# Norm row work on VectorE and ScalarE alone, whole last products, and a mixer that begins with seven gate pairs

## The chip, the cores and the metric

The kernel runs on one core of a Trainium2 chip. The time is device microseconds of one execution; a kernel's time is the median of its runs. Engines are named as in the profile: PE (TensorE matmul), PEld (its weight load), DVE (VectorE), ACT (ScalarE), POOL (GpSimd) and SP (SyncE, which issues most DMAs).

## The reference

One layer on x of 1 x 1024 tokens x 1024 (float32), cut to what is computed:

```python
def rms_norm(x, g):
    y = x * lax.rsqrt(jnp.mean(x * x, axis=-1, keepdims=True) + EPS)
    return y * g

def swiglu_ffn(x, w_in, w_out):                  # D_FF = 2816
    gate, up = jnp.split(x @ w_in, 2, axis=-1)
    return (jax.nn.silu(gate) * up) @ w_out

x = x + 0.5 * swiglu_ffn(rms_norm(x, ffn1_norm), ffn1_w_in, ffn1_w_out)
u = rms_norm(x, mix_norm)
q_a, k_a, v_a, q_b, k_b, v_b, gate_logits = jnp.split(u @ w_mix_in, SPLITS, axis=-1)
y_a = chunked_band_attention(q_a, k_a, v_a, rel_bias_a)        # 8 heads of 64, band of 576 keys
y_b = diff_attention(q_b, k_b, v_b, t5_bias, lam, ...)         # 4 heads, two softmaxes each, rms_norm
g_a, g_b = jnp.split(jax.nn.sigmoid(gate_logits + b_gate), 2, axis=-1)
merged = g_a * (y_a @ w_branch_a) + g_b * (y_b @ w_branch_b)
x = x + merged @ w_o
x = x + 0.5 * swiglu_ffn(rms_norm(x, ffn2_norm), ffn2_w_in, ffn2_w_out)
out = rms_norm(x, final_norm)
```

## The kernel before

Every float32 operand of a large product is split in two parts, "hi" (an ACT cast, L95) and "lo" (a DVE subtraction, L100), and a product is three matmuls, hi·hi, hi·lo and lo·hi (`mm3`, L124). The large projections use the Strassen-Winograd scheme of seven products of half-size blocks (`PRODUCTS`, L167): the activations' sums are made once per norm, the weights' sums (T1, T2, T3, N4) as they are needed.

The stages, one after the other: norm; FFN1-in (22 `Pair`s of columns, seven products of 12 matmuls each, every matmul 128x512); FFN1-out (`out_projection`: seven products `P1` to `P7`, each over 11 blocks i and 4 token tiles, 132 matmuls); norm; mixer-in (16 pairs, and the two `project_v`); attention (branch A with 8 heads, branch B with 4, the projection of A as a filler); the projection of B; W_o (the same `out_projection`, 4 blocks); norm; FFN2-in; FFN2-out; final norm.

The order on each engine is a list scheduler's: the program text gives the priority, data and free buffers the readiness, and each engine then runs its list in order. Buffers are rings: `raw` (RAW = 6 tiles of 4 KB per partition: weights as loaded, rows x, attention's probabilities), `unit` (WU = 18 tiles of 2 KB: the hi and lo parts, and the rows `xc`), `temp` (TF = 10), `wtemp` (TT = 3); one buffer holds the norm's gain or the tables' rows (tag `gain`).

A norm between two stages (`renorm`, L524) has eight rows of 128 tokens. Rows 0 to 3 are done while the last product of the projection runs (`early`): squares on ACT, the power on POOL (`rsqrt`, L137), the scaling on DVE (L201), then `put`: four PE transposes, an ACT cast and a DVE subtraction. Rows 4 to 7 come with the last product (`late`): the same, and for each row four sums of halves on POOL (`norm1a`, L220 to L223), whose results are transposed (S1, S2, S4); the gain of the right half is multiplied in on POOL (L187). While this lasts, the PE has the "heads" of the next stage: products 0 and 2 of a pair, which need only rows 0 to 3 (A11 and A12). Five pairs are begun that way; then the rest of pair 0 starts with T1·S1, which needs all eight rows. In the mixer the pairs 0 to 7 make queries and keys, the pairs 8 to 15 the gates.

With `by_pairs` (W_o and FFN2-out) the last product goes over the token tiles two by two: all blocks i for tokens 4 and 5, then all again for 6 and 7, so that the first two rows can be finished early. Each weight block is split twice, and the activation block in halves of 128x256 whose subtraction is POOL's (L467). In FFN2-out, `finish2` (L1000 on) does the final norm of rows 0 to 3 during it and of rows 4 to 7 behind it.

`setup` (L576 on) makes the two bias tables: POOL loads ea, negates and stretches it, writes `diag_a` with eight DMAs (L613), then `diag_b` with four and four. All of it is called once, at pair 4 of FFN1-in (L386). FFN_ORDER (L398) is the order of the seven products of FFN-out.

Of the kernel before, what the change touches and what calls it, by code (L numbers as in the profile page):

```python
# [9 lines left out]
F32 = mybir.dt.float32  # L10
# [34 lines left out]
RAW, WU, TF, TT = 6, 18, 10, 3  # L45
# [7 lines left out]
def hybrid_layer_kernel(ctx, tc, x, ffn1_norm, ffn1_w_in, ffn1_w_out, mix_norm, w_mix_in,  # L53
# [33 lines left out]
    junk = const.tile([P, HALF], mybir.dt.bfloat16, name="junk")  # L87
# [59 lines left out]
    def rstd_row(xt):  # L147

        ssq = small.tile([P, 2], F32, tag="ssq", name="ssq")
        for d in range(2):  # L150
            nc.scalar.activation(out=junk, in_=xt[d], func=AF.Square,
                                 scale=D ** -0.5, accum_out=ssq[:, d:d + 1])
        v = small.tile([P, 1], F32, tag="v", name="v")
        nc.vector.scalar_tensor_tensor(out=v, in0=ssq[:, 0:1], scalar=EPS, in1=ssq[:, 1:2],
                                       op0=ALU.add, op1=ALU.add)
        return rsqrt(v)

# [16 lines left out]
    class Row:  # L174


        def __init__(self, x):
            self.x, self.gained = x, [None, None]
            self.ssq = small.tile([P, 2], F32, tag="rsq", bufs=10, name="rsq")

        def take(self, d, gain, on_pool):

            nc.scalar.activation(out=junk, in_=self.x[d], func=AF.Square, scale=D ** -0.5,  # L183
                                 accum_out=self.ssq[:, d:d + 1])
            g = gain[:, d * HALF:(d + 1) * HALF]
            if on_pool:
                nc.gpsimd.tensor_tensor(out=self.x[d], in0=self.x[d], in1=g, op=ALU.mult)  # L187
            else:
                self.gained[d] = g

        def scale(self):
# [5 lines left out]
            for d in range(2):  # L197
                if self.gained[d] is None:
                    nc.scalar.activation(out=self.x[d], in_=self.x[d], func=AF.Copy, scale=r)
                else:  # L200
                    nc.vector.scalar_tensor_tensor(out=self.x[d], in0=self.x[d], scalar=r, in1=self.gained[d],  # L201
                                                   op0=ALU.mult, op1=ALU.mult)
# [8 lines left out]
    def norm0(t, row0, u, ps):  # L211

        for d, name in enumerate(("A11", "A12")):
            put(u, name, t, row0.x[d], ps)

    def norm1a(t, row0, row1, u, ps):

        (a11, a12), (a21, a22) = row0.x, row1.x
        s1 = temp([P, HALF], "s1")
        nc.gpsimd.tensor_tensor(out=s1, in0=a21, in1=a22, op=ALU.add)  # L220
        nc.gpsimd.tensor_tensor(out=a21, in0=a11, in1=a21, op=ALU.subtract)
        nc.gpsimd.tensor_tensor(out=a11, in0=s1, in1=a11, op=ALU.subtract)
        nc.gpsimd.tensor_tensor(out=a12, in0=a12, in1=a11, op=ALU.subtract)  # L223
        put(u, "S1", t, s1, ps)
        put(u, "S2", t, a11, ps)
        put(u, "S4", t, a12, ps)

    def norm1b(t, row1, u, ps):

        put(u, "S3", t, row1.x[0], ps)  # L230
        put(u, "A22", t, row1.x[1], ps)
# [22 lines left out]
    class Combine:  # L254


        def __init__(self, ps, shape, sink):
            self.ps, self.shape, self.sink, self.held, self.chains = ps, shape, sink, {}, {}

        def acc(self, m):  # L260

            name = PRODUCTS[m][2]
# [8 lines left out]
        def after(self, m, p):  # L271
# [9 lines left out]
            if m in (0, 1, 3):  # L281
# [14 lines left out]
    class Pair:  # L296
# [4 lines left out]
        def __init__(self, w, c1, c2, u, ps, sink):  # L301
            self.w, self.c, self.u = w, (c1, c2), u
            self.sums = Combine(ps, [P, HALF], sink)
            self.todo = list(range(len(PRODUCTS)))

# [34 lines left out]
    def ffn_in(w_in, u, ps, extra=None):  # L340
# [67 lines left out]
    def out_projection(w_out, operand, order, loads, scale, x_src, x_dst, ps, by_pairs,  # L408
# [638 lines left out]
```

## Time and profile before

| | |
|---|---|
| median of 3 runs | 2211.55 us (2211.3 to 2213.83) |
| profiled execution, its own time | 2213.29 us |
| its span | 2211.5 us |
| granted TensorE clock, mean | 0.981 |
| PE busy | 2096.8 us, 95% |
| DVE busy | 1472.5 us, 67% |
| ACT busy | 991.6 us, 45% |
| POOL busy | 319.7 us, 14% |

The span is what the profile covers; the profiled execution's own time is 1.79 us longer. PE is the engine that the time follows; what it does not work is spread over a few places, which the windows of the trace show (busy time of each engine in a stretch, and the clock granted in it). A mean over the span tells little: DVE is busy 67% on the whole, but in some stretches all the time.

### The profile page before, as it was taken

To read this page: it belongs to the slowest core of one execution; us is meant where nothing else is said; L and a number is where in the kernel's file an instruction comes from. 1 tells how busy PE (TensorE), PEld (TensorE's weight loads), DVE (VectorE), ACT (ScalarE), POOL (GpSimd) and SP (SyncE) were. 2 spreads that over 40 slices of the span, in tenths; PEclk is the share of its full clock that TensorE was granted. 3 is DMA by queue.
4 is the path that set the end of the run, shared out by engine and by line. 5 is a ranking of instruction groups with operands and counts; after the bars stand their busy time and mean duration, and the time that the engine had idled before them with its cause. 6 is when DMAs were issued, how large, how long until landed. Compare 5 with 4: busy or idle time off the path is not lost. (4 is left out here: it accounts for less than half of the span.)

```text
span 2211.5 us, 29192 instructions
## 1 busy us (share of the span) xinstructions
PE 2096.8 (95%) x10025; PEld 1744.8 (79%) x10025; DVE 1472.5 (67%) x2632; ACT 991.6 (45%) x1985; POOL 319.7 (14%) x392
## 2 busy tenths in 40 slices
PE   6999999999999899999999988898999999999996
PEld 5778888888887699888778877686778888888884
DVE  6755656577578755654388977688866655667566
ACT  6423333334446444444388755236533333334435
POOL 6230000000015000000066323215200000000004
PEclk9999999999999899999999998999999999999998
DMA  5473323285354445432596565624433332375324
GB/s 174 121 191 116 118 92 115 100 300 171 115 167 138 149 154 174 164 132 91 155 223 147 140 173 145 236 84 152 138 104 111 113 102 96 119 279 192 114 86 159
DMA packets 274005, 323.36 MB, mean 146 GB/s; under 512 B 16844, under 2 KB 170204, under 8 KB 273856
## 3 DMA queue, kind: packets, MB, share of 16 engines
q1 hardware_dynamic: 269648, 313.58, 45.6%
q0 software_dynamic: 4064, 7.39, 1.5%
q8 instruction: 79, 1.29, 0.2%
q14 instruction: 70, 0.57, 0.1%
q10 hardware_dynamic: 144, 0.52, 0.1%
HBM read 223.11 MB, written 98.30 MB: 145 GB/s over the span
## 5 line engine op out<-in xcount | busy, mean ns | idle before, releaser
L127 PE MATMUL po<-wlo,whi 128*128 128x512 f32 x728 | 287.2, 395 | 14.2 <-DVE wlo L100 14.1
L128 PE MATMUL po<-whi,wlo 128*128 128x512 f32 x728 | 285.3, 392 | 0.0
L100 DVE TENSOR_TENSOR wlo<-raw,whi 128x512 fp32r<-128x512 f32 x200 | 150.7, 755 | 169.5 <-PE prod L127 109.9
L95 ACT CAST whi<-T 128x512 fp32r<-128x512 f32 x196 | 122.1, 623 | 301.1 <-PE prod L127 185.7
L126 PE MATMUL po<-whi 128*128 128x512 f32 x728 | 254.9, 392 | 1.3 <-ACT junk L183 1.2
L95 ACT CAST whi<-raw 128x512 fp32r<-128x512 f32 x200 | 124.0, 622 | 254.6 <-PE prod L127 189.5
L100 DVE TENSOR_TENSOR wlo<-B,whi 128x512 fp32r<-128x512 f32 x193 | 137.9, 717 | 137.2 <-ACT whi L95 137.2
L95 ACT CAST whi<-B 128x512 fp32r<-128x512 f32 x193 | 119.9, 621 | 243.1 <-PE po L127 216.4
L100 DVE TENSOR_TENSOR wlo<-T,whi 128x512 fp32r<-128x512 f32 x196 | 137.6, 702 | 106.7 <-ACT whi L95 77.5
L111 DVE TENSOR_TENSOR c<-prod,c 128x512 f32<-128x512 f32 x192 | 131.6, 687 | 100.8 <-PE prod L128 79.6
L127 PEld LDWEIGHTS po<-wlo,whi 128*128 128x128 f32 x728 | 137.9, 189 | 48.0 <-DVE wlo L100 19.6
L126 PEld LDWEIGHTS po<-whi 128*128 128x128 f32 x728 | 137.0, 189 | 30.6 <-ACT junk L183 1.4
L128 PEld LDWEIGHTS po<-whi,wlo 128*128 128x128 f32 x728 | 137.9, 189 | 28.1
L95 ACT CAST whi<-ha 128x512 fp32r<-128x512 f32 (+1 forms) x165 | 96.9, 587 | 48.5 <-PE prod L127 19.3
L274 ACT COPY c<-prod 128x512 f32<-128x512 f32 x192 | 104.0, 591 | 11.9 <-DMA hA<-c 8.3
L100 DVE TENSOR_TENSOR wlo<-ha,whi 128x512 fp32r<-128x512 f32 x143 | 99.0, 692 | 14.3 <-ACT whi L95 12.4
L100 POOL TENSOR_TENSOR wlo<-ha,whi 128x256 fp32r<-128x256 f32 x22 | 20.7, 949 | 600.6 <-ACT whi L95 596.1
L780 ACT ACTIVATE pm<-pm,mn 128x640 f32<-128x640 f32 (+7 forms) x128 | 94.1, 736 | 14.3 <-DVE mn L778 13.0
L126 PE MATMUL prod<-S3h,whi 128*128 128x512 f32 x240 | 95.0, 396 | 5.7 <-ACT c L274 5.0
L111 DVE TENSOR_TENSOR T<-raw 128x512 f32<-128x512 f32 x128 | 92.7, 726 | 7.8 <-DMA raw<-in_w_mix_in_dram 5.8
L126 PE MATMUL prod<-S1h,whi 128*128 128x512 f32 x240 | 95.8, 399 | 1.6 <-ACT gate L372 0.9
L126 PE MATMUL prod<-A11h,whi 128*128 128x512 f32 x240 | 95.1, 396 | 2.2 <-DVE c L111 1.2
(253 smaller groups left out, 5502.1 us busy)
## 6 DMA issues: line engine op xcount, KB each, us to landing
raw<-in_ffn_w_in_dram SPq DMA_DIRECT2D x98, 512.0 KB, 3.9
raw<-in_w_mix_in_dram SPq DMA_DIRECT2D x45, 512.0 KB, 4.1
ha<-hS SPq DMA_DIRECT2D x88, 256.0 KB, 2.7
hA<-c SPq DMA_DIRECT2D x66, 256.0 KB, 2.2
ha<-hA SPq DMA_DIRECT2D x55, 256.0 KB, 3.1
B<-in_ffn_w_out_dram SPq DMA_DIRECT2D x12, 1024.0 KB, 5.6
hS<-hs SPq DMA_DIRECT2D x44, 256.0 KB, 2.1
hS<-c SPq DMA_DIRECT2D x44, 256.0 KB, 2.8
```

Of the source, the lines that this page charges most:

```text
L95: nc.scalar.copy(out=hi, in_=src)
L100: (nc.gpsimd if on_pool else nc.vector).tensor_tensor(out=lo, in0=src, in1=h, op=ALU.subtract)
L111: nc.vector.tensor_tensor(out=out_, in0=a, in1=b, op=op)
L126: nc.tensor.matmul(ps, a[0], b[0], start=first, stop=False, skip_group_check=shared)
L127: nc.tensor.matmul(ps, a[0], b[1], start=False, stop=False, skip_group_check=shared)
L128: nc.tensor.matmul(ps, a[1], b[0], start=False, stop=last, skip_group_check=shared)
L274: nc.scalar.copy(out=self.held[name], in_=p)
L780: nc.scalar.activation(out=dst, in_=dst, func=AF.Exp, bias=mn, scale=-1.0, accum_out=rs)
```

## The change

1. **Row work.** The gain's multiplication and the four sums of `norm1a` go from POOL to DVE (`add`, L111); POOL keeps the power. Rows 0 to 3 are squared and scaled whole (128x1024). For rows 4 to 7 of the later norms the right half is squared and multiplied by the gain as soon as its product is done (`take_right`); at the end the left half is squared and scaled on DVE, the right scaled on ACT (`scale_halves`). The first norm's rows 4 to 7 are scaled whole as well.
2. **No token pairs.** The last product of W_o and FFN2-out runs over all four tiles at once, as FFN1's does, each operand split once, its subtractions on DVE; `late` comes after it. The final norm runs in place and stores from there.
3. **Mixer.** The gate pairs 2 to 6 come first, with the pairs 0 and 1 of the gates begun ahead of them: seven heads instead of five. The first two ("spill") keep product 0 in SBUF, which frees its PSUM bank. Then queries and keys, the last gate pair at the end; `project_v` follows the pairs at places 10 and 11.
4. **Tables.** `setup` is a generator of four pieces, called at the pairs 5, 8, 11 and 14.
5. **Rings.** RAW 6 to 10, WU 18 to 10 (the same bytes); `xc` is a whole raw tile; `dg` 3 to 2.

```diff
-RAW, WU, TF, TT = 6, 18, 10, 3
+RAW, WU, TF, TT = 10, 10, 10, 3
...
-            if on_pool:
-                nc.gpsimd.tensor_tensor(out=self.x[d], in0=self.x[d], in1=g, op=ALU.mult)
...
+        def scale(self, gain):
+            v = small.tile([P, 1], F32, tag="v", name="v")
+            nc.vector.tensor_scalar(out=v, in0=self.ssq[:, 0:1], scalar1=EPS, scalar2=None, op0=ALU.add)
+            nc.vector.scalar_tensor_tensor(out=self.x, in0=self.x, scalar=rsqrt(v), in1=gain,
+                                           op0=ALU.mult, op1=ALU.mult)
+        def take_right(self, gain):
+            self.take(1)
+            r = self.x[:, HALF:]
+            add(r, r, gain[:, HALF:], ALU.mult)
+        def scale_halves(self, gain):
...
+            left, right = halves(self.x)
+            nc.scalar.activation(out=right, in_=right, func=AF.Copy, scale=r)
+            nc.vector.scalar_tensor_tensor(out=left, in0=left, scalar=r, in1=gain[:, :HALF],
+                                           op0=ALU.mult, op1=ALU.mult)
...
-        nc.gpsimd.tensor_tensor(out=s1, in0=a21, in1=a22, op=ALU.add)
-        nc.gpsimd.tensor_tensor(out=a21, in0=a11, in1=a21, op=ALU.subtract)
-        nc.gpsimd.tensor_tensor(out=a11, in0=s1, in1=a11, op=ALU.subtract)
-        nc.gpsimd.tensor_tensor(out=a12, in0=a12, in1=a11, op=ALU.subtract)
+        add(s1, a21, a22)
+        add(a21, a11, a21, ALU.subtract)
         put(u, "S1", t, s1, ps)
+        add(a11, s1, a11, ALU.subtract)
+        add(a12, a12, a11, ALU.subtract)
...
-            if m in (0, 1, 3):
+            if self.spill and m == 0:
+                hold("p1")
+            elif self.spill and m < 4:
...
+                add(self.held[name], p, self.held["p1"])
...
-            if j == 4 and extra:
+            if extra and j in (5, 8, 11, 14):
                 with tc.issue_after(silu[-1].ins):
-                    extra(ps)
+                    next(extra, None)
...
-                    rows[1][t][dh] = sb.tile([P, HALF], F32, tag="w", bufs=WU, name="xc")
+                    whole[t] = whole[t] or raw_tile([P, D], "xc")
+                    rows[1][t] = halves(whole[t])
...
-                n = 2 if by_pairs else 4
-                for t0 in range(0, 4, n):
-                    for i in range(nk):
-                        a = split_units(operand(an, i, slice(t0 * P, (t0 + n) * P)), on_pool=by_pairs)
-                        w = split_units(weight(bn, i) if t0 == 0 else blocks["B21", i])
...
+            if m == len(order) - 1 and last:
+                early()
...
+                if th:
+                    (mid if dh else late)(whole)
...
+            for t in range(4):
+                nc.sync.dma_start(out=x_dst[4 + t][:, :HALF], in_=rows[t][:, :HALF])
+                row1[t].take(0)
+                row1[t].scale_halves(gain)
+                for _ in range(1 + extra_heads * (t == 0)):
+                    next(projection, None)
+                norm1a(t, row0[t], row1[t], u, ps)
...
-            pairs += [Pair(w_mix, GATE + j * P, GATE + D + j * P, u2, ps, gate_sink(j)) for j in range(KT)]
-            for p in pairs[:5]:
+            pairs += [Pair(w_mix, GATE + j * P, GATE + D + j * P, u2, ps, gate_sink(j), j < 2) for j in range(KT)]
+            for p in pairs[8:15]:
                 p.head()
                 yield
-            for n, p in enumerate(pairs):
+            for n, p in enumerate(pairs[10:15] + pairs[8:10] + pairs[:8] + pairs[15:]):
                 p.rest()
-                if n in (3, 4):
+                if n in (10, 11):
...
-        def finish2(t, xt):
-            o = raw_tile([P, D], "o")
-            r = rstd_row(xt)
...
+        def late2(rows):
+            for t in range(4):
+                row1[t].take(0)
+                row1[t].scale_halves(gain_f)
+                finish2(4 + t, row1[t])
```

How the order of the instructions moves, at three places. The first is the norm between FFN1-out and the mixer. Before, POOL has the four sums of a row there, `xc` being a row of tokens 4 to 7 and `xt` one of 0 to 3:

```order
L137 TENSOR_TENSOR r<-v,neg_half 128x1 x8
L220 TENSOR_TENSOR s_5899<-xc 128x512
L221 TENSOR_TENSOR xc<-xt,xc 128x512
L222 TENSOR_TENSOR xt<-s_5899,xt 128x512
L223 TENSOR_TENSOR xt<-xt 128x512
```

In the change DVE has them, between the second head's sum (`c`, with the spilled product `p`) and the parts of the next weights:

```order
L111 TENSOR_TENSOR c_5895<-prod,p_5876 128x512
L100 TENSOR_TENSOR wlo<-raw,whi 128x512
L111 TENSOR_TENSOR s_5940<-xc 128x512
L100 TENSOR_TENSOR wlo<-raw,whi 128x512
L111 TENSOR_TENSOR xc<-xt,xc 128x512
L111 TENSOR_TENSOR xt<-s_5940,xt 128x512
L111 TENSOR_TENSOR c_5918<-prod,c_5918 128x512
L111 TENSOR_TENSOR xt<-xt 128x512
```

POOL's four sums a row now stand in DVE's one list, among the weight parts that PE waits for; the queries' second rounding (L102, one a head) is gone from that list, since gates need none.

The second place is DVE at the end of FFN2-out. Before, behind the first token pair (`o` is the scaled row, `B` the weight block, split a second time):

```order
L474 SCALAR_TENSOR_TENSOR xc<-po,xc 128x512
L100 TENSOR_TENSOR wlo<-B_19167,whi 128x512
L1005 SCALAR_TENSOR_TENSOR o<-xt,r,gain 128x512 x2
L100 TENSOR_TENSOR wlo<-B_19167,whi 128x512 x2
L154 SCALAR_TENSOR_TENSOR v<-ssq 128x1
```

In the change, the end of the list (`ha` is the activation block):

```order
L100 TENSOR_TENSOR wlo<-B_19273,whi 128x512
L100 TENSOR_TENSOR wlo<-ha,whi 128x512
L492 SCALAR_TENSOR_TENSOR xc<-po,xc 128x512 x4
L191 SCALAR_TENSOR_TENSOR v<-rsq 128x1 x3
L196 SCALAR_TENSOR_TENSOR xc<-xc,r,gain 128x512
L191 SCALAR_TENSOR_TENSOR v<-rsq 128x1
L196 SCALAR_TENSOR_TENSOR xc<-xc,r,gain 128x512 x3
```

The second split of the weights and the rows in between are gone; all four rows of tokens 4 to 7 are finished behind the last matmul.

The third is POOL's list from the tables on. Before:

```order
L617 DMA ea<-in_rel_bias_a_dram 128x1x257
L584 TENSOR_SCALAR ea<-ea 128x257
L619 COPY ea<-ea 128x511
L613 DMA diag_a<-ea 8x16x768 x8
L584 TENSOR_SCALAR eb<-tb 128x640
L613 DMA diag_b<-eb 4x32x640 x4
```

In the change:

```order
L607 DMA ea<-in_rel_bias_a_dram 128x1x257
L573 TENSOR_SCALAR ea<-ea 128x257
L609 COPY ea<-ea 128x511
L602 DMA diag_a<-ea 8x16x768 x8
L573 TENSOR_SCALAR eb<-tb 128x640
L602 DMA diag_b<-eb 4x32x640 x4
```

Nothing has come between them: POOL's list reads the same, and the four pieces hold no new wait.

## Rows read from the trace of the kernel before

**Rows 1.** The page's part 1: busy time (share of the span) and instructions of each engine.
```profile
PE 2096.8 (95%) x10025; PEld 1744.8 (79%) x10025; DVE 1472.5 (67%) x2632; ACT 991.6 (45%) x1985; POOL 319.7 (14%) x392
```

**Rows 2.** The waits of PE: engine, operation, line, releaser: total us, times, longest.
```profile
PE po L127 <- DVE wlo L100: 14.1, 11, 3.3
PE sc L770 <- DMA ks<-k: 11.0, 2, 5.9
...
PE tr L208 <- DVE S4l L100: 9.4, 3, 5.8
```

**Rows 3.** Windows: start:end, length, busy us (instructions) by engine, clock, DMA share, GB/s.
```profile
24.90:66.20 41.30, 36.40 (x166) 28.86 (x165) 33.11 (x41) 23.21 (x44) 28.78 (x21) 0.99 0.42 125
110.00:130.00 20.00, 15.54 (x57) 12.31 (x56) 9.17 (x16) 4.53 (x8) 4.58 (x5) 0.83 0.94 265
660.00:687.90 27.90, 27.90 (x141) 23.26 (x140) 22.46 (x40) 19.17 (x43) 2.99 (x4) 1.00 0.33 105
687.90:735.00 47.10, 35.18 (x161) 28.20 (x159) 40.38 (x50) 22.42 (x44) 27.37 (x20) 0.88 0.58 180
...
1510.00:1573.30 63.30, 51.92 (x245) 39.81 (x245) 60.69 (x80) 41.48 (x90) 42.82 (x35) 0.97 0.44 136
...
2155.60:2202.20 46.60, 36.22 (x133) 25.97 (x131) 33.23 (x45) 26.25 (x65) 22.74 (x26) 0.93 0.49 167
2202.20:2211.50 9.30, 0.00 (x0) 0.00 (x0) 3.89 (x8) 2.89 (x8) 1.09 (x2) 0.68 0.30 113
```
In these rows the engines stand in the order PE, PEld, DVE, ACT, POOL.

**Rows 4.** PE's timeline, the mixer's first head and the 48th matmul: start, us, instruction.
```profile
687.87 0.39 PE L126 MATMUL prod<-A11h,whi 128*128 128x512 f32 x1
...
698.52 0.39 PE L128 MATMUL prod<-A12h,wlo 128*128 128x512 f32 x1
```

**Rows 5.** DVE's timeline in FFN2-out's last product and behind it.
```profile
2154.47 2.48 DVE L501 SCALAR_TENSOR_TENSOR x<-po,x 128x512 f32<-128x512 f32 x4 [0.24 <-PE po L128]
...
2164.82 2.35 DVE L1005 SCALAR_TENSOR_TENSOR o<-xt,r,gain 128x512 f32<-128x512 f32 x2 [0.67 <-POOL r L137]
2167.09 1.81 DVE L100 TENSOR_TENSOR wlo<-B,whi 128x512 fp32r<-128x512 f32 x2
...
2207.00 1.41 DVE L1005 SCALAR_TENSOR_TENSOR o<-xc,r,gain 128x512 f32<-128x512 f32 x2 [0.66 <-POOL r L137]
```

**Rows 6.** DVE's groups, 1573.3 to 1700 us (POOL silent): busy us, mean ns, idle before.
```profile
L100 DVE TENSOR_TENSOR wlo<-raw,whi 128x512 fp32r<-128x512 f32 x16 | 11.0, 686 | 13.0 <-ACT whi L95 6.6 <-PE prod L127 6.4
L111 DVE TENSOR_TENSOR T<-raw 128x512 f32<-128x512 f32 x16 | 10.9, 685 | 0.2
```

**Rows 7.** ACT's timeline behind FFN2-out's last matmul.
```profile
2202.53 0.63 ACT L151 ACTIVATE junk<-xc 128x512 bf16<-128x512 f32 x1 [4.97 <-DVE xc L474]
2203.06 0.19 ACT L151 ACTIVATION_READ_ACCUMULATOR junk<-xc 128x1 f32 x1
```

**Rows 8.** ACT's groups, 687 to 700 us.
```profile
L199 ACT ACTIVATE xc<-xc,r 128x512 f32<-128x512 f32 x4 | 2.7, 712 | 0.0
```

**Rows 9.** PE's timeline between FFN1 and mixer.
```profile
720.24 1.09 PE L208 MATMUL tr<-ident,xt 128*128 128x128 f32 x4 [5.83 <-DVE S4l L100]
```

**Rows 10.** POOL's groups, 690 to 722 us, and DVE's, 690 to 735 us.
```profile
L223 POOL TENSOR_TENSOR xt<-xt 128x512 f32<-128x512 f32 x4 | 6.5, 1620 | 0.3
...
L100 DVE TENSOR_TENSOR wlo<-raw,whi 128x512 fp32r<-128x512 f32 x8 | 8.6, 1079 | 0.0
L102 DVE SCALAR_TENSOR_TENSOR c<-c,qkh 128x512 f32<-128x512 f32 x5 | 6.7, 1344 | 0.1
```

**Rows 11.** DVE's groups, 1510 to 1573.3 us.
```profile
L100 DVE TENSOR_TENSOR wlo<-raw,whi 128x512 fp32r<-128x512 f32 x11 | 13.3, 1222 | 0.4 <-ACT whi L95 0.4
```

**Rows 12.** The timelines of PE and POOL at the tables.
```profile
124.31 0.80 PE L126 MATMUL prod<-S3h,whi 128*128 128x512 f32 x1 [4.46 <-ACT c L274]
...
120.50 1.80 POOL L584 TENSOR_SCALAR eb<-tb 128x640 f32<-128x640 f32 x1 [14.50 <-DMA diag_a<-ea]
```

**Rows 13.** PE's timeline where the fourth head of branch B begins.
```profile
1332.91 0.69 PE L770 MATMUL sc<-ks,qs 128*128 128x128 f32 x2 [5.93 <-DMA ks<-k]
```

**Rows 14.** Groups of attention, 1105 to 1285 us.
```profile
L100 DVE TENSOR_TENSOR wlo<-pt,whi 128x512 fp32r<-128x512 f32 x48 | 32.8, 684 | 10.9 <-ACT whi L95 10.9
...
L95 ACT CAST whi<-pt 128x512 fp32r<-128x512 f32 x48 | 27.9, 582 | 11.7 <-PE pt L786 11.5
```

More of the change, by code (lines that the diff above doesn't have):

```diff
@@ L304, in __init__ @@
             self.todo = list(range(len(PRODUCTS)))
+            self.spill = spill
+            self.sums.spill = spill
         def product(self, m, get):
@@ L416, in out_projection @@
         blocks, banks, begun, complete = {}, {}, set(), set()
-        rows = [[[None, None] for _ in range(4)] for _ in range(2)]
+        rows, whole = [[[None, None] for _ in range(4)] for _ in range(2)], [None] * 4
         def load_block(name, i0, i1):
@@ L493, in out_projection @@
                     prepare(th, dh)
-                if i == (nk - 1) // 2 and m == len(order) - 2 and (1, 0) not in begun:
-                    begun.add((1, 0))
-                    prepare(1, 0)
             done = (th, dh) not in [OUT[o][3:] for o in order[m + 1:]]
@@ L506, in out_projection @@
                 complete.add((th, dh))
-                if th == 0 and (0, 1 - dh) in complete:
+                if th:
+                    (mid if dh else late)(whole)
+                elif (0, 1 - dh) in complete and not last:
                     early()
-                elif th:
-                    mid(rows[1])
     def drams(n, shape, name, dtype=F32):
@@ L530, in early @@
             for t in range(4):
-                row0.append(Row(halves(load(x_dst[t], raw_tile([P, D], "xt")))))
+                row0.append(Row(load(x_dst[t], raw_tile([P, D], "xt"))))
             for t in range(4):
-                for d in range(2):
-                    row0[t].take(d, gain, False)
-                row0[t].scale()
+                row0[t].take()
+                row0[t].scale(gain)
                 norm0(t, row0[t], u, ps)
@@ L634, in hybrid_layer_kernel @@
         gain = load_gain(ffn1_norm[0], nc.scalar)
-        ffn1 = ffn_in(ffn1_w_in[0], u, ps, setup)
+        ffn1 = ffn_in(ffn1_w_in[0], u, ps, setup(ps))
         row0, row1 = [], []
         for t in range(4):
-            row0.append(Row(halves(load(rows(x)[t], raw_tile([P, D], "xt")))))
-            for d in range(2):
-                row0[t].take(d, gain, False)
-            row0[t].scale()
+            row0.append(Row(load(rows(x)[t], raw_tile([P, D], "xt"))))
+            row0[t].take()
+            row0[t].scale(gain)
             norm0(t, row0[t], u, ps)
@@ L644, in hybrid_layer_kernel @@
             next(ffn1, None)
-            row1.append(Row([sb.tile([P, HALF], F32, tag="w", bufs=WU, name="xt") for _ in range(2)]))
-            for d in range(2):
-                load(rows(x)[4 + t][:, d * HALF:(d + 1) * HALF], row1[t].x[d])
-                row1[t].take(d, gain, d == 1)
-            row1[t].scale()
+            row1.append(Row(load(rows(x)[4 + t], raw_tile([P, D], "xt"))))
+            row1[t].take()
+            row1[t].scale(gain)
             norm1a(t, row0[t], row1[t], u, ps)
+        next(ffn1, None)
         for t in range(4):
```

131 lines of the change are left out of this document (54 added, 77 removed).

## The prediction

> **What bounds the kernel now.** I read the page's part 1 first: PE works 2096.8 us, 95% of the span, so some 115 us of idle time are all there is to win, besides what a lowered clock costs [rows 1]. Then the waits of PE: the largest groups are a weight's lo part that DVE has late, the loads of keys in attention, and transposes of norm rows, which wait behind a DVE subtraction [rows 2]. They don't lie in the steady stages, so I took windows of the places where stages meet [rows 3]. In each, PE is short of its window by several us: the start 36.40 of 41.30, the tables' stretch 15.54 of 20.00, the norm between FFN1 and mixer 35.18 of 47.10, the one between W_o and FFN2 51.92 of 63.30, FFN2-out's last product 36.22 of 46.60. Against them stands FFN1-out's last product: 27.90 of 27.90. The sum is made against the profiled execution, 2213.29 us; the median, 2211.55, is 1.74 below it.
>
> **The end (parts 1, 2).** The last product of FFN2-out has 132 matmuls. At full clock one follows another in (698.52 − 687.87) / 47 = 0.2266 us [rows 4], so it needs 29.9; it takes 46.6 [rows 3]. DVE's timeline shows why: a row's two scalings hold it for 2.35 us, and the next weight part waits behind them [rows 5], while a weight serves only six matmuls, 1.36 us. Undivided, each weight serves twelve, 2.72 us, and is split once: 22 subtractions of 0.69 (the time of one with POOL silent, [rows 6]) are 15.2, and four whole rows, each at the 1.41 of two halves [rows 5], 5.6: 21 of 29.9. FFN1-out's last product is that loop with rows 0 to 3 beside it, and never idle [rows 3]. I take the whole difference, **16.7**. Behind PE's end there are 9.3 us now, for two rows [rows 3]. For four: the evacuations are 2.48 / 4 = 0.62 apart [rows 5], begun while the last tiles are still multiplied; a square takes 0.63 [rows 7], so squares keep up, and the last ends some 1.7 behind PE (one evacuation, one square and its read, an estimate from these). Four scalings of 0.71 on ACT [rows 8] end at 4.5; from the last scaling to the span's end it was 2211.5 − 2207.00 − 1.41 = 3.1 [rows 5]. That is 7.6, and I keep 1.4 in hand: **0.3** gained. The end gives 17, between 12 (a lo part late by 1 us in five of the eleven steps) and 18.
>
> The Trainium skill speaks against this part: "Perfetto Trace Analysis", section "Optimizing Scalar/DVE Operations", says that where Scalar or Vector aren't saturated but cause bubbles on others, breaking up instructions may let work be completed sooner, and the token pairs are broken-up work. By it the end would rather lose; rival 2 prices from rows what could be lost. The two windows of the last products say the opposite of the loop itself.
>
> **Between FFN1 and mixer (parts 1, 3).** From the first head at 687.9 to the first T1·S1 at 735.0 PE has five heads, 120 matmuls or 27.2 us, and the puts; its busy 35.18 leaves 8.0 for those [rows 3]. It stops for rows that POOL is adding, the longest time for 5.83 us at 720.24 [rows 9]. POOL's sums take some 1.6 us, 16 of them in a chain, and while POOL runs, DVE's operations on two SBUF operands are long, 1.08 to 1.34 in the mean [rows 10], where they take 0.69 with POOL silent [rows 6]. After: DVE's 40.4 us [rows 3] lose the five second roundings of queries (6.7) and the excess of eight weight parts, 8 x 0.39 = 3.1 [rows 10]; they gain 16 sums at 0.62 (from one start to the next in an unbroken run, [rows 5]), 9.9, and six instructions for two heads, 3.7: 44 at most, since other operations that run long now are left out. PE has seven heads, 168 matmuls or 38.1, and the puts, 8.0: 46.1. So PE is the longer of the two. It has done 48 matmuls more by then, 10.9, so 46.1 stands against 47.1 + 10.9 = 58.0: 11.9, if PE is never idle. Waits may take 1.5 off it; the clock, 0.88 in this window [rows 3], gives about as much back: **12**. Lower end 6: the raw tiles left for weights are two as before, and a weight that is late by one load holds DVE and then PE. Upper end 16: the puts without the lowered clock.
>
> **Between W_o and FFN2 (parts 1, 2).** DVE is the bound here, 60.69 of 63.30 with 80 instructions [rows 3], some of them at 1.22 instead of 0.69 [rows 11]. The change's list for DVE has 17 more between the same ends: 97, eight of them tiny (0.2), four of twice the size. At 0.62 from start to start that is 89 x 0.62 + 4 x 0.62 + 1.6 = 59.3. With the 2.6 that DVE is idle now it is 61.9, without them 4.0 less than now. I take **3**; −1 if each of the 17 comes 0.24 late once, 7 if PE's stall on the pairs' weights, 3.3 (the longest of its kind, [rows 2]), goes as well.
>
> **The start.** POOL has the same 16 sums and four gain products here, 28.78 us of POOL in the window [rows 3], and they move to DVE, which has 8.2 idle. The sums at 0.62 are 12.4; the excess over 0.69 that they cause today gives about as much back, if it is as large as between FFN1 and mixer. PE is idle 4.9 us. I take **2**, between −3 (DVE late by the sums that its idle time doesn't hold) and 5 (no idle left).
>
> **Tables (part 4).** PE stops for 4.46 us at 124.31, because a buffer's store is late behind the table DMAs [rows 12]. Would four pieces spread them? POOL's list in the change reads as before, its first load still waits for the transpose ahead of it, and no other work of POOL lies between; each step begins when the DMAs of the one before are done, as now (14.50 us of waiting, [rows 12]). The pieces come later in the text, not in time. I take **0.5**, between 0 and 6 (4.46, and some of the clock of 0.83 in these 20 us, [rows 3]).
>
> **Rings and attention (part 5).** Ten raw tiles let the scores run further ahead. Two stalls for keys, 11.0 us together [rows 2], fall where the third and fourth head of branch B begin, the fourth's at 1332.91 [rows 13]. In the new list the fourth head's loads come a piece of filler earlier, and more scores and products stand ahead of their first use; the third's cover is about the same. I take two thirds of the 5.93, **4**, between −8 (nine of rival 3's groups, 11.4) and 10 (both stalls). The spill, the mixer's new order and the smaller `dg` ring I cost at nothing: a steady pair's seven products (19 us of PE) cover its some 15 DVE instructions, 10 us at 0.69; without that cover the spill would cost a sum of 0.69, twice.
>
> Sum: 17 + 12 + 3 + 2 + 0.5 + 4 = 38.5. 2213.3 − 38.5 = 2174.8 for an execution like the profiled one, and 2173 for the median.
>
> **Rivals.**
> 1. VectorE becomes the bound: the sums stand in its one list ahead of weight parts that PE waits for, and the two norms, the start and attention give nothing or 1.5 in all: 2211.6 − 18.5 = 2193. For it: DVE has 60.69 of 63.30 in one norm already. Against it: the excess while POOL runs, which goes. 0.16.
> 2. The tail of four rows: if each two rows take what two take now, 9.3 becomes 18.6, and the end gives 7.7: 2182. For it: each row is a chain of square, power, scaling, store. Against it: rows overlap, 0.62 apart. By the skill's rule above it would come out this way. 0.07.
> 3. Slower: ten units starve attention. Place: the transposed probabilities of branch A, each group of four blocks needing a hi and a lo unit, 48 groups of 128x512 in its 180 us [rows 14]. Price: a group without lookahead shows PE its cast and its subtraction, 0.58 + 0.68 = 1.27 [rows 14]; all 48 cost 61: 2173 + 4 + 61 = 2238. It decides from (38.5 − 4) / 1.27 = 27 groups on. For it: 18 units become 10, and a job of A can hold six. Against it: PE's list of transposes and products is nearly the same in both, and FFN1-out's last product ran with ten units (eight held rows) without a gap. 0.05.
> 4. The pieces do spread, as the change says: the stall at 124 and its slow clock go, 6 more: 2167. Against it stands POOL's list. 0.05.
>
> **How the numbers follow.** My forecast has 0.64, the rivals 0.16, 0.07, 0.05 and 0.05; 0.03 is left for gains and losses that cancel. A measurement of this kernel can tell about 0.2%, 4.4 us, from no change. Faster: 0.64 + 0.16 + 0.07 + 0.05 = 0.92; the same 0.03; slower 0.05, rival 3. The terms' bounds don't all fall to one side: the lower ones, by the root of their squares (5, 6, 4, 5, 0.5, 12), are 15, the upper ones (1, 4, 4, 3, 5.5, 6) 10, which is 2163 to 2188. Rival 1 at 2193, with 2 us around it, sets the upper end, 2195; two upper bounds on top, 8, the lower, 2155.
>
> **What would show it.** The end: PE without waits in some 30 us, then 7 to 9 us behind it. FFN1 to mixer: POOL with powers only, DVE's operations at 0.69, T1·S1 some 46 to 48 us behind the first head. W_o to FFN2: DVE without a pause, its operations at 0.69. Tables: the stall near 124 still there. Attention: one stall for keys instead of two, and no new wait on whi or wlo. Wrong would be: DVE's operations at 1.1 to 1.3 with POOL silent, a PE wait on DVE of over 3 us in the mixer's start, or new waits of over 10 us on units in attention.

## The result, and the profile after

The changed kernel takes 2186.07 us in the median (2182.71 to 2190.20, 4 runs) against 2212.69 (2211.30 to 2215.74, 4 runs): a ratio of 0.9879, interval 0.9858 to 0.9899, 26.6 us. The forecast was 2173 with a range of 2155 to 2195. The direction and the range hold; the gain is two thirds of the forecast's, and it is made of other terms.

The profiled execution is the fastest of the four; its span is 2180.9 us, 30.6 less than that of the one profiled before, so its stages below add up to 30.6 and not to 26.6. Its page, part 1 (compare [rows 1]):

```profile
PE 2081.4 (95%) x10025; PEld 1734.5 (80%) x10025; DVE 1462.8 (67%) x2678; ACT 976.9 (45%) x1911; POOL 199.1 (9%) x302
```

POOL has lost 120 us of work and DVE has not grown. In this sum other parts of the change stand too (run 4, without token pairs alone, has DVE at 1457.4); run 6 below takes the sums by themselves. The largest waits of PE (compare [rows 2]):

```profile
PE prod L126 <- ACT c L270: 11.7, 2, 9.5
PE tr L203 <- DVE xt L179: 9.3, 1, 9.3
PE sc L761 <- DMA kl<-k: 7.3, 3, 3.6
...
PE sc L760 <- DMA ks<-k: 7.1, 3, 3.5
PE po L127 <- DVE wlo L100: 6.1, 9, 1.5
```

The waits for a weight's lo part have fallen from 14.1 to 6.1, those for S4 and S2 rows are gone from the top; a wait on a sum (`c`) of 9.5 us and waits for keys have taken their place. Windows of the same places as in [rows 3] (start:end, length, busy us of PE, PEld, DVE, ACT, POOL, clock, DMA share, GB/s):

```profile
24.10:59.55 35.45, 34.70 (x165) 28.39 (x165) 31.51 (x56) 18.90 (x35) 1.68 (x3) 1.00 0.32 90
100.00:125.00 25.00, 14.98 (x56) 11.56 (x55) 9.18 (x15) 4.66 (x8) 4.58 (x5) 0.80 0.95 235
...
687.90:731.50 43.60, 42.88 (x210) 35.49 (x208) 37.33 (x65) 28.69 (x53) 2.85 (x4) 1.00 0.63 192
...
2139.00:2169.40 30.40, 29.84 (x131) 24.04 (x129) 19.72 (x32) 14.93 (x29) 4.13 (x4) 1.00 0.48 173
2169.40:2180.90 11.50, 0.02 (x1) 0.00 (x0) 4.29 (x10) 4.77 (x12) 2.48 (x4) 0.61 0.48 184
```

The norm into the mixer is now PE's own, 42.88 of 43.60 with 168 head matmuls instead of 120; the last product takes 31.0 instead of 46.6 (its first matmul starts at 2138.45, just ahead of the window); the tables' stretch has become worse. DVE's operations in the norm into the mixer, 688 to 731 us (compare [rows 10]):

```profile
L100 DVE TENSOR_TENSOR wlo<-raw,whi 128x512 fp32r<-128x512 f32 x12 | 8.2, 688 | 4.4 <-ACT whi L95 4.4
...
L111 DVE TENSOR_TENSOR s<-xc 128x512 f32<-128x512 f32 x4 | 2.7, 686 | 0.0
```

1.08 us a weight part has become 0.69 with POOL all but silent (2.85 of 43.60), and a sum that took POOL 1.5 to 1.6 takes DVE 0.69.

The span in seven stages, in us, read from the start of the first instruction of each kind in PE's timeline (T1·S1 is the first product that needs all rows):

| | before | after | gain | forecast |
|---|---|---|---|---|
| start to FFN1's first T1·S1 | 66.2 | 59.5 | 6.6 | 2 |
| to the mixer's first head | 621.7 | 628.4 | −6.7 | 0.5 (tables) |
| to attention's first scores | 419.1 | 400.2 | 18.9 | 12 |
| to attention's last transposed row | 286.4 | 287.8 | −1.4 | 4 |
| to FFN2's first T1·S1 | 179.9 | 177.9 | 2.0 | 3 |
| to the end of PE | 628.9 | 615.6 | 13.3 | 16.7 |
| to the span's end | 9.3 | 11.5 | −2.1 | 0.3 |

Three signs are wrong: tables, attention, tail. The runs below go after them, and after who earned the rest.

### The profile page after: what moved, and what is told of

It is laid out like the page before. It is cut to its first block, busy times and chain, and to the rows that moved or that the text cites. A ratio compares the mean times of both kernels' runs of the same rounds, so it can differ in the third digit from the quotient of the medians.

```text
span 2180.9 us, 28950 instructions
## 1 busy us (share of the span) xinstructions
PE 2081.4 (95%) x10025; PEld 1734.5 (80%) x10025; DVE 1462.8 (67%) x2678; ACT 976.9 (45%) x1911; POOL 199.1 (9%) x302
## 4 chain that ended last, share of the span: by engine, by line
PE 36%; DVE 5%; DMA 4%; ACT 3%; issue 2%; SPq 0%; POOL 0%; ACTq 0%; DVEq 0%; POOLq 0%
PE prod L126 6%; PE prod L127 6%; PE prod L128 6%; PE po L127 3%; PE po L128 3%; PE po L126 3%; DVE wlo L100 1%; DMA kl<-k 1%; PE pt L776 1%; ACT whi L95 1%; PE sc L760 1%; PE pb L126 1%; PE pb L128 1%; PE pb L127 1%; ACT pm L770 1%
## 5 line engine op out<-in xcount | busy, mean ns | idle before, releaser
L111 DVE TENSOR_TENSOR c<-prod,c 128x512 f32<-128x512 f32 x190 | 131.2, 691 | 148.4 <-PE prod L128 130.5
L95 ACT CAST whi<-B 128x512 fp32r<-128x512 f32 x178 | 110.8, 622 | 266.2 <-PE po L127 258.3
L100 DVE TENSOR_TENSOR wlo<-raw,whi 128x512 fp32r<-128x512 f32 x200 | 138.8, 695 | 103.8 <-ACT whi L95 64.5
L100 DVE TENSOR_TENSOR wlo<-B,whi 128x512 fp32r<-128x512 f32 x178 | 123.0, 691 | 126.4 <-ACT whi L95 126.3
L126 PE MATMUL po<-whi 128*128 128x512 f32 x728 | 198.1, 391 | 0.4 <-ACT whi L95 0.4
L137 POOL TENSOR_TENSOR r<-v,neg_half 128x1 f32<-128x1 f32 x64 | 51.6, 810 | 1306.4 <-DVE v L178 1210.3
L100 DVE TENSOR_TENSOR wlo<-N,whi 128x512 fp32r<-128x512 f32 x64 | 44.2, 690 | 112.9 <-PE prod L127 66.6
L100 DVE TENSOR_TENSOR wlo<-ha,whi 128x512 fp32r<-128x512 f32 x154 | 106.0, 689 | 9.0 <-ACT whi L95 9.0
L770 ACT ACTIVATE pm<-pm,mn 128x640 f32<-128x640 f32 (+7 forms) x128 | 94.0, 736 | 22.7 <-DVE mn L768 12.7
L95 ACT CAST whi<-ha 128x512 fp32r<-128x512 f32 x154 | 94.8, 615 | 16.9 <-PE prod L127 11.4
L768 DVE CUSTOM_DVE_ANT_0 pm<-sc,nb 128x640 f32<-128x640 f32 (+7 forms) x128 | 88.5, 699 | 20.2 <-PE sc L761 19.4
```

The costliest lines, as they stand in the source:

```text
L95: nc.scalar.copy(out=hi, in_=src)
L100: (nc.gpsimd if on_pool else nc.vector).tensor_tensor(out=lo, in0=src, in1=h, op=ALU.subtract)
L111: nc.vector.tensor_tensor(out=out_, in0=a, in1=b, op=op)
L126: nc.tensor.matmul(ps, a[0], b[0], start=first, stop=False, skip_group_check=shared)
L137: nc.gpsimd.tensor_tensor(out=r, in0=v, in1=neg_half, op=ALU.pow)
L768: nc.vector.tensor_tensor_reduce(out=d3, in0=sc, in1=nb.rearrange("p (n w) -> p n w", n=n), scale=1.0, scalar=3e38, op0=ALU.add, op1=ALU.m ...
```

## The experiments

The kernel before was timed again beside each group of runs: 2210.6 us beside runs 1 to 4, 2210.5 beside 5 to 8, 2210.1 beside 9 and 10, 2208.8 beside 11. Ratios are to these. The stages come from one profiled execution of each kernel; where two kernels are the same up to a stage, they show how far it varies.

**1. Fewer weights ahead.** Edit, on the changed kernel:

```diff
-RAW, WU, TF, TT = 10, 10, 10, 3
+RAW, WU, TF, TT = 6, 10, 10, 3
...
+    def row_tile(shape, name):
+        return sb.tile(shape, F32, tag="row", bufs=4, name=name)
...
-                    whole[t] = whole[t] or raw_tile([P, D], "xc")
+                    whole[t] = whole[t] or row_tile([P, D], "xc")
...
-            row1.append(Row(load(rows(x)[4 + t], raw_tile([P, D], "xt"))))
+            row1.append(Row(load(rows(x)[4 + t], row_tile([P, D], "xt"))))
```

> The changed kernel with its ring of ten raw tiles divided: six for weights and attention's probabilities, as before the change, and four for the rows xc (and for rows 4 to 7 of the first norm). Theory A: ten raw tiles let SP queue more weight loads ahead of the stores, so the stores of hidden blocks land late (4.3 us in the median instead of 2.2), and PE's stall at the tables grew from 4.5 to 9.5 us for that; then the stall is at most 5 here, the stores land in 2 to 3 us, the 2.2 us wait in FFN2's third pair goes, and the time falls by 5 to 9 us, to some 2179. Rival B: the stall grew because the table DMAs now start 10 us earlier against the pairs' stores; then it stays at 8 to 10 us and the time within 3 us of the changed kernel's 2186. Attention, first scores to last transposed row: 287.8 us with the change, 286.4 before; if the raw ring made it longer it is 286 here, if the units did it stays at 288.

Measured: 2185.35 us, ratio 0.9885 (0.9861 to 0.9909). The stall at the tables is 11.3 us, FFN2's 2.1, and stores of hidden blocks land in 4.3 us as in the change: theory A is wrong. The ten raw tiles had not caused the stall. Rival B's time fits, but its stall of 8 to 10 us doesn't quite, and this run doesn't show its reason. Two other things came with the tiles: the start is back at 65.0 (59.5 in the change), so by this run most of the start's unforeseen gain was the deeper ring and not the norm; and attention takes 286.1.

**2. Tables that do lie apart.** A value from each pair's gate is added, times zero, into the table before two of its DMAs:

```diff
+                    if extra and th:
+                        z = small.tile([P, 1], F32, tag="tick", name="tick")
+                        nc.gpsimd.tensor_tensor(out=z, in0=dst[:, :1], in1=zero, op=ALU.mult)
+                        ticks.append(z)
...
-            if extra and j in (5, 8, 11, 14):
-                with tc.issue_after(silu[-1].ins):
-                    next(extra, None)
+            if extra and j >= 5:
+                next(extra, None)
...
+                if c % 2 == 0:
+                    yield
+                    hold(src)
                 nc.gpsimd.dma_start(out=diag[:, c * r:(c + 1) * r, e0:e1], in_=src)
+        def hold(t):
+            nc.gpsimd.tensor_tensor(out=t[:, :1], in0=t[:, :1], in1=ticks[-1], op=ALU.add)
```

> The changed kernel with table pieces that do lie apart in time: each pair of FFN1-in from the sixth on releases, through a value taken from its result, one step (the load of ea, or two of the sixteen table DMAs). Theory: the stall of 9.5 us near 119 is the table DMAs' burst, so no wait of PE over 1 us is left between 100 and 400 us, and with the clock that falls behind the stall 10 to 13 us are won: 2173 to 2176. Rival: the stall comes from the weight loads alone, or two table DMAs in a pair suffice to delay a store; then waits of 2 to 5 us show up in several pairs and the time falls by less than 5.

Measured: 2176.72 us, ratio 0.9850 (0.9830 to 0.9870), 9.3 less than the change, and than run 3 beside it. That is just short of the theory, which left no wait over 1 us. POOL's timeline shows the pieces apart, two DMAs a pair:

```profile
171.55 0.52 POOL L614 TENSOR_TENSOR ea<-ea,tick 128x1 f32<-128x1 f32 x1
172.37 1.29 POOL L611 DMA_DIRECT2D diag_a<-ea  x2 [0.30 <-POOL ea L614]
190.41 0.19 POOL L386 TENSOR_TENSOR tick<-gate,zero 128x1 f32<-128x1 f32 x1 [16.75 <-ACT gate L383]
```

PE's wait at that place, in the change and here, and the change's wait at the same place of FFN2, where no table is made:

```profile
119.41 0.79 PE L126 MATMUL prod<-S3h,whi 128*128 128x512 f32 x1 [9.54 <-ACT c L270]
...
1604.94 0.51 PE L126 MATMUL prod<-S3h,whi 128*128 128x512 f32 x1 [2.21 <-ACT c L270]
```

```profile
111.74 0.50 PE L129 MATMUL prod<-S3h,whi 128*128 128x512 f32 x1 [2.21 <-ACT c L273]
```

So 7.3 us of the stall was the tables' burst, and the change's "four pieces" had not broken it up: there POOL issues the eight DMAs of `diag_a` in one go at 91.3 us, as before at 101.1. What is left is 2.2 us, the same in FFN1 and FFN2, at the same instruction: something that the change made in both.

**3. Whole-row stores at the end.**

```diff
-            for d, xt in enumerate(halves(row.x)):
-                nc.sync.dma_start(out=out[t * P:(t + 1) * P, d * HALF:(d + 1) * HALF], in_=xt)
+            nc.sync.dma_start(out=out[t * P:(t + 1) * P, :], in_=row.x)
```

> The changed kernel with one store of a whole row in the final norm instead of two of half rows. Theory: behind the last matmul SP's issue of eight stores (4.5 us for them) bounds the end; with four, the span ends 7.5 to 8.5 us behind the last matmul instead of 11.5, and the time falls by 3 to 4. Rival: the landing of the last 2 MB bounds it; then it ends 10.5 us or more behind, and the time falls by at most 1.

Measured: 2186.04 us, ratio 0.9894 (0.9873 to 0.9915); 11.5 us behind the last matmul, as in the change. The rival is right. The DMA view of that run, its stretch from 2172 us to the end in 40 slices (busy tenths, GB/s):

```profile
DMA  0000000000000009999999999999999910000000
GB/s 0 0 0 0 0 0 0 0 0 0 0 0 0 0 0 403 389 376 430 390 430 363 389 416 430 416 403 390 416 416 389 389 40 27 0 0 0 0 0 0
DMA packets 577, 2.11 MB, mean 173 GB/s; under 512 B 64, under 2 KB 64, under 8 KB 576
```

Four issues or eight, the DMA engines are full, and 2.11 MB at some 400 GB/s take 5.3 us; they begin only when the first row is scaled, and the span ends some 2 us after them.

**4. Only the token pairs undone, in the kernel before.** The edit: `by_pairs` False in the calls for W_o and FFN2-out.

> The kernel before with one part of the change alone: no token pairs in the last product of W_o and of FFN2-out. Theory: FFN2-out's last product takes 30 us instead of 46.6, the end behind the last matmul 10 to 14 instead of 9.3 (four rows, sixteen half-row operations on DVE, eight stores), W_o to the first T1 S1 of FFN2 changes by less than 3: a gain of 12 to 16 us against the kernel before, 2197 to 2201. Rival: without the row work taken off POOL the loop stays held up by DVE, 35 us or more for the last product, and the gain is under 8.

Measured: 2197.30 us, ratio 0.9940 (0.9917 to 0.9963), 13.3 less than before. From FFN2's first T1·S1 to PE's end 610.5 us (628.9 before), the tail 12.7, W_o's norm unchanged at 180.2. The theory holds, and with it the first term of the sum: FFN2 gives 18 us here (its last product takes 30.1), less 3.4 in the tail. It also shows what FFN2 can be: 610.5, five less than in the change, with the old rings.

**5. The rings undone.** All of the change but part 5 (the `dg` ring stays at 2); the first norm's rows 4 to 7 lie in units too, and are scaled by halves for that:

```diff
-RAW, WU, TF, TT = 10, 10, 10, 3
+RAW, WU, TF, TT = 6, 18, 10, 3
...
-                    whole[t] = whole[t] or raw_tile([P, D], "xc")
+                    whole[t] = whole[t] or pair_tile("xc")
...
+            row1.append(Row(pair_tile("xt")))
...
+            row1[t].take_right(gain)
+            row1[t].scale_halves(gain)
```

> The changed kernel with part 5 undone: six raw tiles, eighteen units, the rows xc as two units. Its list for PE begins the rest of the first FFN pairs one after another again (T1 S1 products at the 0th, 48th, 120th, 144th, 192nd matmul), where ten units interleave five of them (0, 48, 108, 132, 146, 167, 180). Theory: the interleaving holds so many sums in the ten temporary buffers that the next one waits for a store of a hidden block; then the wait in FFN2's third pair (2.2 us, 4.2 with the clock) is 1.5 or less here and the one at the tables 4 to 6 instead of 9.5, and the start loses 5 us, as with six raw tiles alone: 2182 to 2186. Rival: the wait is the table DMAs' and the stores' own and stays as in the change, 9 us and 2.2: 2188 to 2192.

Measured: 2169.91 us, ratio 0.9815 (0.9800 to 0.9829): 16 us less than the change by the medians, 14 by the ratios, 13.1 between the profiled executions: far below what I had expected. FFN2 has no wait on a sum at all; stores land in 2.5 us instead of 4.3. The stall at the tables is 6.7. Part 6 of the page, DMA issues (count, KB each, median us to landing), of the change and of this run:

```profile
hA<-c SPq DMA_DIRECT2D x66, 256.0 KB, 4.3
```

```profile
hA<-c SPq DMA_DIRECT2D x66, 256.0 KB, 2.5
```

The stages tell where the rest is: attention's end to FFN2's first T1·S1 170.7 us instead of 177.9, FFN2 611.3 instead of 615.6, FFN1 624.5 instead of 628.4, attention 284.6 instead of 287.8; the start loses 3.3 and the mixer 2.2. Against run 1, which has six raw tiles too, W_o's stage is 6.4 shorter and the FFNs 4.6 and 4.7: by this comparison it is the units. The windows of W_o's stage, of the change and of this run:

```profile
1375.97:1553.87 177.90, 164.75 (x726) 131.21 (x727) 142.86 (x229) 72.61 (x135) 20.20 (x17) 0.97 0.44 145
```

```profile
1374.40:1545.10 170.70, 163.54 (x723) 132.90 (x723) 141.42 (x227) 72.86 (x135) 23.36 (x17) 0.96 0.48 162
```

Each engine does the same work; PE is idle 13.1 us in the one and 7.2 in the other. The difference lies mostly in short waits for DVE. PE's waits in that window, of the change:

```profile
PE po L127 <- DVE wlo L100: 3.3, 3, 1.5
PE tr L203 <- DVE A11l L100: 2.7, 1, 2.7
...
PE tr L203 <- DVE S1l L100: 1.8, 1, 1.8
```

and of this run, whose list has no wait for S1l:

```profile
PE tr L207 <- DVE A11l L100: 1.5, 1, 1.5
PE po L127 <- DVE wlo L100: 1.2, 1, 1.2
```

**6. The sums on POOL again**, all else as in the change (`norm1a` with `nc.gpsimd.tensor_tensor` for its four `add`s).

> The changed kernel with the sixteen sums of each norm on POOL again, as before the change; all else as in the change. Theory: DVE's operations become long again while POOL adds, and PE waits for the sums: from the mixer's first head to attention 410 us or more instead of 400, the start's first T1 S1 at 64 instead of 59.5, FFN2's head to T1 S1 41 or more instead of 38; 12 to 20 us slower than the change, 2198 to 2206. Rival: seven heads cover the sums wherever they are made; then these stretches stay within 3 us each and the time within 5 of 2186.

Measured: 2194.25 us, ratio 0.9918 (0.9902 to 0.9935), 8.2 slower than the change: between the two. DVE's weight parts are long again in the norm into the mixer:

```profile
L100 DVE TENSOR_TENSOR wlo<-raw,whi 128x512 fp32r<-128x512 f32 x12 | 14.0, 1168 | 2.3 <-ACT whi L95 2.3
```

but its stretch to T1·S1 grows by 3.4 only, which fits seven heads covering the rest, the start by 2.6, and W_o's stage (181.2) lies in the spread of the other runs with ten units (177.1 to 182.7). This profile also has the longest attention of all, 293.6, where no norm's sums are made; its cause is open. The page's part 1 shows what the sums are to DVE:

```profile
PE 2089.3 (95%) x10025; PEld 1740.8 (79%) x10025; DVE 1453.1 (66%) x2630; ACT 976.9 (44%) x1911; POOL 269.0 (12%) x350
```

In the change DVE has 48 sums more, 33 us at 0.69, and is busy only 9.7 longer: the rest is won back on its other operations.

**7. Five heads, queries first**, all else as in the change (`pairs[:5]` and `enumerate(pairs)`, no spill, `project_v` after pairs 3 and 4, no extra heads).

> The changed kernel with part 3 undone: queries and keys first, five heads, no spill. Theory: DVE is the longer engine without the two heads: from the mixer's first head to attention, which took 400.2 us with the change and 419.1 before, 406 to 410; 6 to 10 us slower than the change, 2192 to 2196. Rival: the sums on DVE do it alone and the heads are worth 3 us or less: 2186 to 2189.

Measured: 2198.52 us, ratio 0.9943 (0.9928 to 0.9958), 12.5 slower, more than the theory's 6 to 10. The mixer from its first head to attention takes 409.7 us, as the theory said; 9.4 of the mixer's 18.9 us are part 3's. The time left over, about 3, lies in attention and W_o's stage, whose spread it doesn't leave.

**8. Tables spread, and the last two blocks by token pairs.** To run 2 is added, in FFN2-out's last product:

```diff
-                for t in range(4):
-                    mm3(banks[chain][t], [v[:, t * P:(t + 1) * P] for v in a], w,
-                        first and i == 0, i == nk - 1, not first)
+                held.append((i, a, w))
...
+                elif i == nk - 1:
+                    mm = tokens(0, 2)
+                    with tc.issue_after(mm.ins):
+                        tokens(2, 4)
```

> The changed kernel with tables spread as in the run before, and with the last two of the eleven blocks of FFN2-out's last product taken by token pairs: tokens 4 and 5 for both blocks, then 6 and 7, with the same split operands. Theory: the span's end is bound by writing 2.1 MB at 390 GB/s behind the last scaling; half of it can go 2.7 us earlier, so 8 to 9 us lie behind the last matmul instead of 11.4, and with the tables the time is 2172 to 2175. Rival: the four rows' chain on ACT bounds it and the order gains nothing: 11 us behind, 2176 to 2178.

Measured: 2174.29 us, ratio 0.9837 (0.9818 to 0.9855); 9.45 us behind the last matmul, 2.0 less than in the change. Half of the output leaves early; what remains is the last two rows' chain and their stores. The time is 2.4 below run 2's, and their intervals overlap: the gain is read from the tail, not from the time.

**9. The three gains together**: the rings of run 5, the tables of run 2, the end of run 8.

> Parts 1 to 4 of the change with the rings of before (six raw tiles, eighteen units, as in the run with the rings undone, 2170), with the tables spread and the last two blocks by token pairs. Theory: the three gains are in different stages and add: the wait of 6.7 us at the tables and the clock behind it go (8), the end is 2 shorter: 2159 to 2162. Rival: a store of a hidden block is late for its own sake with the tables gone too, as it was with ten units (2.2 us left at the tables' place), and the spread gives 4 or less: 2163 to 2167.

Measured: 2160.32 us, ratio 0.9775 (0.9761 to 0.9790), 26 less than the change (23 by the ratios) and 50 less than before. From FFN1's first T1·S1 to the mixer 616.8 us instead of 624.5 in run 5, the tail 9.35 instead of 11.4: they add. PE at the tables' place, run 5 and this run:

```profile
124.63 0.80 PE L126 MATMUL prod<-S3h,whi 128*128 128x512 f32 x1 [6.72 <-ACT c L274]
```

```profile
117.32 0.50 PE L129 MATMUL prod<-S3h,whi 128*128 128x512 f32 x1 [0.97 <-ACT c L277]
```

**10. Seven raw tiles, sixteen units**, else as run 9.

> The same with seven raw tiles and sixteen units. Theory: units are what counts, through the order that the scheduler makes of them and through lookahead in W_o, and sixteen less eight for the rows xc leave eight there, fewer than the ten of before: from the last transposed row of attention to FFN2's first T1 S1 173 to 178 us instead of 170.7, FFN2 612 to 615 instead of 611.3, 2 to 8 us slower than with six and eighteen; the start is 1 to 3 us shorter for the raw tile. Rival: two units more or less change nothing: within 2 us.

Measured: 2165.99 us, ratio 0.9806 (0.9790 to 0.9823), 5.7 slower than run 9, but not where the theory put it: W_o's stage is 170.4 and FFN2 612.0, both as with eighteen. The start is 2.5 longer, where the theory had it shorter for the raw tile, and attention 2.8. Sixteen units are enough in W_o's stage; where between ten and sixteen it begins to cost was not tried.

**11. Run 9 with the sums on POOL.**

> The fastest kernel so far (six raw tiles, eighteen units, tables spread, last two blocks by token pairs) with the sixteen sums of each norm on POOL. In the change itself the sums' move was worth 8 us, and nothing in the norm between W_o and FFN2. Theory: there the ten units hid it; with eighteen that norm shows it: from the last transposed row of attention to FFN2's first T1 S1 177 to 181 us instead of 171.2, the start 2 to 4 longer, the mixer from its first head to attention 3 to 5 longer; 12 to 18 us slower, 2172 to 2178. Rival: the sums' move is worth nothing after W_o in any rings, and the 9.5 us between the run without pairs and the run with the rings undone came from the row work taken whole: 171 to 173 there, 5 to 9 us slower in all, 2165 to 2169.

Measured: 2176.46 us, ratio 0.9856 (0.9839 to 0.9872), 16.1 slower than run 9. W_o's stage takes 178.6 instead of 171.2, the start 69.0 instead of 61.2, the norm into the mixer 46.8 instead of 43.6. The theory holds, but for the start, which loses 7.7 where it had 2 to 4: with enough units the move of the sums is worth twice what it is in the change, and with ten units none of it shows in W_o's stage.

## Why the prediction was right or wrong

**The end's loop** was right in mechanism and size: 31.0 us for the last product where I said some 30, and runs 4 and 5 have 30.1 with either placing of the row work. FFN2 as a whole gave 13.3, because it lost 2.2 earlier (the wait on a sum, below). **The end's tail** was wrong in sign. I followed the chain of the last row up to its scaling, which came out right (some 4.8 us behind PE, forecast 4.5), and then added the 3.1 us of the kernel before. That number held for a store of one row; four rows at once are 2.11 MB, and run 3 shows the DMA engines full for 5.3 us. The failing step is the term "from the last scaling to the span's end": 3.1 forecast, 6.7 measured. Rival 2 had the direction and another reason, the chains of rows. Run 8, which breaks up only the last two blocks, wins 2.0 us without a second split. The rule of the Trainium skill that stood beside rival 2 ("Perfetto Trace Analysis", section "Optimizing Scalar/DVE Operations": breaking up instructions may let work be completed sooner) is thus borne out by the traces in the tail (9.3 us by token pairs, 12.7 when run 4 takes them out) and not in the loop (31.0 us unbroken, 46.6 by token pairs).

**FFN1 to mixer** was right in mechanism, too small in size: 14.5 at equal work (47.2 + 10.9 − 43.6) for the 11.9 worked out, because the 8.0 us I gave to the puts held the lowered clock (0.88) too: at 1.00, in the change, 42.88 − 38.1 = 4.8 are left for them. Another 4.4 came behind T1·S1, which no run takes apart. Run 7 gives 9.4 to the heads and the order, run 11 3.2 to the sums in the stretch to T1·S1.

**Between W_o and FFN2** I forecast 3 and 2.0 came, but that agreement is a coincidence. The 2.0 isn't clear of the stage's own spread (run 3, the same kernel up to its last stores, takes 180.5 there, the change 177.9, the kernel before 179.9), and two larger amounts stand behind it: with eighteen units the row work gives 9.5 (180.2 in run 4, 170.7 in run 5), of which run 11 gives 7.4 to the sums, and ten units take 7.2 of them back.

**Rings and attention** is the step that failed. I took the rings for free and gave attention 4 us for ten raw tiles; run 5 shows that part 5 costs 13 to 16 us in all, and without it the change gives 40.6 us, where my sum without attention's 4 was 34.5; term by term that is no agreement either (FFN1 −2.8, W_o 9.2 for 3). I had priced scarce units in one place alone, the transposed probabilities of attention (rival 3), and dismissed them for the out-projections because FFN1's last product ran with ten. But an operand ring of ten did two other things. It changed the list: with ten units the scheduler interleaves the first pairs of each FFN, and PE meets a product whose sum has no buffer until a store has landed (2.2 us and the clock behind it in FFN2, and 9.5 with the tables' burst in front of the same store). The products' places in the list move with the units and not with the raw tiles (run 1 has the change's interleaving, run 5 that of before), and the wait in FFN2 goes with them. All seven kernels with ten units have that wait in FFN2, 1.9 to 2.3 us, and none with more. But the interleaving isn't enough to explain it: run 10, with sixteen units, interleaves these pairs too (T1·S1 at the 0th, 48th, 110th, 142nd, 158th, 177th matmul) and has no such wait. The stores differ as well: a store of a hidden block (hA) lands in 4.1 to 4.3 us in the median with ten units, 3.5 with sixteen, 2.2 to 2.7 with eighteen. How many of the ten temporary buffers were held at that moment I did not count, so the link from the units to the wait is argued. And it left W_o's stage idle for 6 us more, in the waits on DVE that stand under run 5. In attention the two stalls for keys stayed, as six shorter waits, 14.4 us in all where they had taken 11.0; three of them:

```profile
1266.67 0.41 PE L760 MATMUL sc<-ks,qs 128*128 128x128 f32 x2 [3.38 <-DMA ks<-k]
1269.53 0.66 PE L761 MATMUL sc<-kl,qs 128*128 128x128 f32 x2 [2.21 <-DMA kl<-k]
...
1316.42 0.66 PE L761 MATMUL sc<-kl,qs 128*128 128x128 f32 x2 [3.60 <-DMA kl<-k]
```

Attention takes 284.5 to 288.3 us in the six kernels with six raw tiles and 287.6 to 293.6 in the seven with more. The deeper ring did not help there: run 1, which differs from the change in it alone, has the two stalls as before (11.5 us, the longer 6.0), and its attention is 1.7 shorter, within the spread of the kernels above.

**Tables.** That the pieces would not lie apart was right, and run 2 shows what they are worth when they do, 9.3 us (forecast as rival 4: 6). That the stall would stay as it was, was not: it grew from 4.5 to 9.5. Run 5 has 6.7, so the rings account for some 3 of it; the other 2 came with parts 1 to 4, and no run says from which.

**The start** gave 6.6 for 2. By run 1, 5.4 of it are the raw tiles, a cause that I had not considered. But runs 5 and 9, with six raw tiles and eighteen units, start in 62.9 and 61.2, and run 10, with seven and sixteen, in 63.8: the tiles' share lies between 1.7 and 5.4, and the stage varies by over 1 us. By run 11 the sums are worth more there (7.7) where the ring is short. The change also begins the fifth head of FFN1 ahead of the last puts, which my list of its parts left out and no run tests.

Rival 1 (VectorE becomes the bound) did not come: in the norm into the mixer DVE's weight parts fell to 0.69 us, and DVE is busy 37.33 of 43.60.

Two slips in the prediction's last sums move nothing: the lower bounds as listed have a root of 15.7, not 15, and in rival 2 the end would give 7.4, not 7.7, since its 0.3 would be gone.

## What to carry to other kernels

Work for one engine's spare time isn't free when it lengthens another's instructions: moving POOL's sums to a busy DVE won back 23 of the 33 us that the sums added to it. A ring's size is part of the order: when a list scheduler plans around buffers, build the list with the new size and compare it, stage by stage, before taking the ring for neutral; and try the rest of a change with the old rings. At a kernel's end, price the bytes that become ready together as well as the last row's chain.

## What the runs showed of the hardware that I had not expected

Behind the last matmul eight stores of 256 KB or four of 512 KB took the same time (11.5 and 11.4 us to the span's end), at 355 to 430 GB/s with all DMA engines busy; issuing them (4.5 us against 2.9 us of SP) did not matter. And in the change eight table DMAs of 384 KB issued in one go lay beside stores of 256 KB on another queue that took 12.0 us to land (median of two, 100 to 122 us); with two at a time (run 2, 165 to 200 us) such a store took 5.5 us. The burst isn't all of it: in the kernel before, with the same eight, two such stores took 7.2 us.
